# Layer 1's last four output weights: multiplied in the head before the last, and only split in the last one

## The chip, the cores and the metric

The kernel runs on one core of a Trainium2 chip. The metric is the device time of one execution in microseconds (us); less is better. Engines are named as the profile names them: PE (TensorE), DVE (VectorE), ACT (ScalarE), POOL (GpSimd), SP (SyncE, which issues nearly all DMAs here).

## What is computed

Two layers over 1024 latent tokens and 256 context tokens of width 1024. Layer 0 is multi-head latent attention with 16 heads; layer 1, where the change is, is differential attention with 8 heads: each head has two softmaxes over the same values, and the second is subtracted.

```python
def combine(o1, o2, gate):
    o = o1 - lam_full.astype(o1.dtype) * o2
    o = rms_norm(o, g_sub) * (1.0 - lambda_init)
    return gated(o, gate)                    # o * silu(gate)
...
x = layer_norm(DEEPNORM_ALPHA * x + gate[:, None, :] * (o @ out_w[i]), ln_g[i], ln_b[i])
```

In layer 1 only the latent tokens are put out. `gate`, the row behind the attention, is a vector over the 1024 output columns, and g_sub one over the 128 rows of a head's piece of the output weights. So both can be multiplied into the output weights: row k of the weights (128 x 1024, the rows that belong to head k) becomes out_w[k] * gsub * gate1, where gsub is one number per partition and gate1 the gate, repeated on all partitions.

## The kernel before

**Accuracy.** Products are made of split operands: a value is kept as a high part and a low part, and a product is three matmuls (L185 to L187: high by high, low by high, high by low). `split` (L176, L177) casts the high part on ACT and subtracts it on a second engine, DVE or POOL, for the low part; `split16` (L181, L182) does the same in 16 bits with a scale: ACT writes `ph`, `vh`, `kH`, DVE writes `pl`, `vl`, `kL`.

**Layer 1 in heads and tiles.** The loop over the heads h = 0 to 7 runs eight tiles t of 128 queries. A step of a tile computes its scores (`scores1`: matmuls L1338/L1339 into PSUM banks, maxima L1351/L1355 on DVE, six exponentials L1361 on ACT into p0 and p1, then sums and the difference of the softmaxes, L1364 to L1367, on DVE), turns the p of the tile before (`turn1`: transposes L1374, then `split16` into ph and pl) and multiplies the tile before that with the values (`values1`: L1382 to L1384, then o, o2 at L1387/L1388 on ACT, a norm on POOL, and a store of o by SP). Eight PSUM banks "b" are shared by all of it.

**Side work.** Between these pieces a generator G makes the next head's operands: K and Q (`prod_k1`, `prod_q1`, with the buffers rsw, kr, kH, kL, cosB, sinB), V and the head's gate columns (`prod_v1`, with rr, Vf and gg: copies L1316/L1318 from the banks, `split16` of Vf into vh and vl, the silu of gg at L1323, which loads another ACT table, and its store sg_d at L1324), and the next weights. In head 6, the last but one, no weights are left to make; there V of head 7 is woven with rows 0 to 3 of the output weights (`out_w1`): a DMA loads a row into ws (L1421), DVE multiplies it by gsub and gate1 (L1423), and `split` makes the parts oH1k and oL1k.

**The last head.** Before head 7's first tile `out_open` closes the pool a1proj, which holds all the buffers of K, Q, V and the gate, and opens a1out in its place: gb3 (a row of the layer norm), g, res and z (two buffers each), bs and mv. Then it loads gb2 and gb3, takes the space of the layer's input (bigA, bigB) for the parts of rows 4 to 7 ("o1" and "o2" in the trace, `o` where numbers are left out), reads back a tile's o and gate and multiplies them (`out_load`, L1450 to L1452), and for k = 4 to 7 loads a row into z or res (L1421), multiplies it on DVE (L1423) and splits it (ACT L176, POOL L177). In head 7's steps G makes the output of earlier tiles instead: transposes of o (`out_turn`, L1464, split into wx and wy), the product with all eight rows (L185 to L187 with oH, oL), the layer norm and the store. Its first two steps have no such side work.

**What sets the order.** PE executes its instructions in the order of the code. On DVE, ACT, POOL and SP the order is set by the scheduler of the framework, as the rows further down show; every engine, SP's DMA queue too, works through its own order strictly, so that an instruction that waits holds all behind it. A buffer of a closed pool can be written again only when its last readers are done.

Of the kernel before, what the change touches and what calls it, by code (L numbers as in the profile page):

```python
# [17 lines left out]
P = 128  # L18
# [35 lines left out]
def hybrid_kernel(  # L54
# [909 lines left out]
    def bcast_row(dst, src):  # L964
        sp.dma_start(dst, src.to_broadcast([P, D]))
# [9 lines left out]
    def w1(tag):  # L975
        sh, d, b = TAG1[tag]
        return rot(place[tag], sh, d, tag, b)
# [70 lines left out]
    with ow_ctx, spool("o0") as op0:  # L1048
# [96 lines left out]
        for t in range(8):  # L1145
# [53 lines left out]
            "ss": ([P, 2], F32, 2)}  # L1199

    TAGP = {"cosB": ([P, SEQ], F32, 1), "sinB": ([P, SEQ], F32, 1), "rsw": ([P, 512], F32, 1),
            "rr": ([P, 512], F32, 1), "kr": ([P, NTOK], F32, 1),
            "kH": ([P, NTOK], F16, 1), "kL": ([P, NTOK], F16, 1), "gg": ([P, SEQ // P, P], F32, 1),
            "Vf": ([P, NT, P], F32, 1)}

    TAGO = {"gb3": ([P, D], F32, 1), "g": ([P, D], F32, 2), "res": ([P, D], F32, 2), "z": ([P, D], F32, 2),
            "bs": ([P, 2, 6], F32, 2), "mv": ([P, 4], F32, 2)}
    for k_, v_ in TAGL.items():
        rot(wl, v_[0], v_[1], k_, v_[2], first=True)
    prj = ExitStack()  # L1210
    wp = prj.enter_context(spool("a1proj"))
    for k_, v_ in TAGP.items():
        rot(wp, v_[0], v_[1], k_, v_[2], first=True)
# [3 lines left out]
    wo4 = a1.enter_context(spool("a1ow", side="right"))  # L1217
    oHL = [[wo4.tile([P, D], F32R, name=f"oH1{k}"), wo4.tile([P, D], F32R, name=f"oL1{k}")] for k in range(NOW)]
    gate1 = wo4.tile([P, D], F32, name="gate1")
    cosB, sinB = w1("cosB"), w1("sinB")  # L1220

    sp.dma_start(cosB, cs1[0])
# [2 lines left out]
    def weave(main, side, at):  # L1225

        for i, v in enumerate(main):
            if i in at:
                next(side, None)
            yield v  # L1230
        yield from side
# [170 lines left out]
    def gate_row1():  # L1402

        pool.memset(gate1, 0.0)
        sp.dma_start(gate1[0:1, :], ada_b[1:2, 2 * D:3 * D])
        for k in range(KT):
            w = w1("ws")
            sp.dma_start(w, ada_w[1, k * P:(k + 1) * P, 2 * D:3 * D])
            yield 0
            dve.scalar_tensor_tensor(gate1, w, sc[:, 2 * k:2 * k + 1], gate1, op0=ALU.mult, op1=ALU.add)  # L1410
            yield 0
        for c0 in (0, 512):
            bk = bank("b")
            pe.matmul(bk, ones, gate1[:, c0:c0 + 512], start=True, stop=True)
            act.copy(gate1[:, c0:c0 + 512], bk)
            yield 2048

    def out_w1(k, ws_of):

        ws = ws_of()  # L1420
        sp.dma_start(ws, out_w[1, k * P:(k + 1) * P, :])  # L1421
        yield
        dve.scalar_tensor_tensor(ws, ws, gsub, gate1, op0=ALU.mult, op1=ALU.mult)  # L1423
        split(oHL[k][0], oHL[k][1], ws, e_lo=pool)
        yield

    def out_open():

        prj.close()
        wo = a1.enter_context(spool("a1out"))  # L1430
        place.update({k_: wo for k_ in TAGO})
        TAG1.update(TAGO)
        for tag, home, src in (("gb2", "wsq", ln_g), ("gb3", "gb3", ln_b)):
            og[tag] = w1(home)
            bcast_row(og[tag], src[1:2, :])
        rest = [big.tile([P, 5, D], F32R, tag=tg, name=nm("o1")) for tg in ("bigA", "bigB")]
        oHL.extend([r[:, k - NOW, :] for r in rest] for k in range(NOW, KT))
        out_load(0)
        for k in range(NOW, KT):
            z = [w1("z"), w1("res")][k % 2]  # L1440
            for _ in out_w1(k, lambda: z):
                pass
            if k == NOW:
                out_load(1)

    def out_load(t):
# [85 lines left out]
    with tc.manual_schedule(engines={ENG[c] for c in MAN1}):  # L1532
        for _ in prod_q1(0, 0, made.pop("q")):
            pass
        later.pop()()
        for _ in chain(prod_k1(0, made), prod_q1(0, 1),
                       weave(prod_v1(0), prod_w(1, 0), WAT[1])):
            while later:
                later.pop(0)()
        joined, turned = [], []  # L1540

        def step1(cur, side, at):

            with tc.high_priority(HP):
                if cur:
                    S = scores1(*cur)
                    next(S)
            some(side, at[0])
            with tc.high_priority(HP):
                if cur:  # L1550
                    next(S)
                if turned:
                    values1(*turned.pop(0))
            some(side, at[1])
            pc = None
            if joined:
                c_, pc, sm = joined.pop(0)
                ph, pl = w1("ph"), w1("pl")
                turned.append((*c_, ph, pl, sm))
            for (k0, n), v in zip(((0, 4), (4, 4), (8, 2)), at[2:]):  # L1560
                if pc is not None:
                    with tc.high_priority(HP):
                        turn1(pc, ph, pl, k0, n)
                some(side, v)
            if cur:
                with tc.high_priority(HP):
                    joined.append((cur, *next(S)))
            for _ in range(len(later)):
                later.pop(0)()

        g1 = gate_row1()
        part = lambda: (v for _, v in zip(range(4), g1))
        for h in range(H1):
            last = h == H1 - 1
            if not last:
                G = chain(weave(weave(chain(prod_k1(h + 1), prod_q1(h + 1, 0), prod_q1(h + 1, 1)), part(), (1, 9, 17, 25)),
                                prod_w(h + 1, 1), WAT[0]),
                          weave(prod_v1(h + 1), prod_w(h + 2, 0) if h + 2 < H1 else
                                chain(*[out_w1(k, lambda: w1("ws")) for k in range(NOW)]),
                                WAT[1] if h + 2 < H1 else range(1, 40, 4)))  # L1580
            else:
                while later:
                    later.pop(0)()
                out_open()
            for t in range(SEQ // P):
                if last:
                    if t >= 2:
                        out_load(t)
                    G = weave(out_tile1(t - 2), out_turns(t - 1), (9, 12)) if t >= 2 else iter(())
                    if t == 2:  # L1590
                        G = chain(out_turns(0), G)
                    credit[0] = 0
                step1((h, t), G, SLOT1 if not last else SLOTO)
                if last:
                    for _ in G:
                        pass
            for _ in G:
                pass
        for t in range(SEQ // P - 2, SEQ // P):
            G = weave(out_tile1(t), out_turns(t + 1), (9, 12))  # L1600
            credit[0] = 0
            step1(None, G, SLOTO)
            for _ in G:
                pass
# [74 lines left out]
```

## Time and profile before

| | |
|---|---|
| median of 3 runs | 1797.15 us (1794.52 to 1799.22) |
| the profiled execution's own time | 1797.62 us |
| its span in the profile | 1795.8 us (1.8 us lie outside it) |
| mean granted PE clock | 0.988 |
| PE, DVE, ACT, POOL busy | 93%, 69%, 62%, 44% of the span |
| head 6, V of head 7 woven in | about 1586 to 1624 us |
| head 7, the stage of the change | from 1624.6 us |
| first output product of head 7 in full flow | from 1659.5 us |

Rows of the trace give start and duration in us, engine, line, operation, out<-in by the program's names; behind them in brackets stands how long the engine was idle before, and what ended that. Rows of the waits give the waiting engine, tile and line, what it waited for, total, times and longest. Rows of the stretches give, per engine, busy us and instructions, then granted PE clock, DMA share and GB/s.

### The profile page before, as it was taken

The page shows a single profiled execution, that of the slowest core. Times are in us where ns is not written, and L with a number is a line of the kernel's source. Part 1 is how long each engine was busy: PE and PEld are TensorE (multiplying, and loading weights), DVE is VectorE, ACT ScalarE, POOL GpSimd, SP SyncE. Part 2 cuts the span into 40 slices and gives each one's busy share as a digit, 9 for nine tenths or more (in the row PEclk, how much of TensorE's full clock was granted, in tenths as well). Part 3 has the DMA queues.
Part 4 walks back from the last instruction along what each step waited for, and adds up shares of the span by engine and source line. Part 5 has one row for each costly group of instructions (what it writes and reads, how often), then busy time and mean ns, then how long its engine had stood idle before and what let it go on. Part 6 is the DMA issues. An engine that isn't in the chain of part 4 may idle for free. (4 is left out here: it accounts for less than half of the span.)

```text
span 1795.8 us, 36757 instructions
## 1 busy us (share of the span) xinstructions
PE 1668.3 (93%) x14564; PEld 1237.5 (69%) x14564; DVE 1236.9 (69%) x2047; ACT 1117.9 (62%) x2233; POOL 796.3 (44%) x722
## 2 busy tenths in 40 slices
PE   7999989999999998999999999989999999986998
PEld 7999955656666565577866666767676757574876
DVE  7658566566665757557746777787778777979564
ACT  3541167877777787835536676767675766666442
POOL 1422136767776676845541222222314131435454
PEclk9999999999999999999999999999999999998999
DMA  8258520110111112164432213121212122223331
GB/s 304 80 156 256 164 56 23 44 44 21 42 46 34 43 44 81 51 217 161 148 117 74 58 54 79 55 78 54 68 41 64 35 68 58 62 61 124 101 116 70
DMA packets 111225, 154.84 MB, mean 86 GB/s; under 512 B 13415, under 2 KB 84679, under 8 KB 111054
## 3 DMA queue, kind: packets, MB, share of 16 engines
q1 hardware_dynamic: 102654, 144.90, 27.3%
q10 hardware_dynamic: 8400, 7.61, 1.3%
q8 instruction: 114, 1.87, 0.4%
q14 instruction: 57, 0.47, 0.1%
HBM read 98.65 MB, written 27.07 MB: 70 GB/s over the span
## 5 line engine op out<-in xcount | busy, mean ns | idle before, releaser
L779 POOL TENSOR_TENSOR pl<-p,ph 128x1024 f16<-128x1024 f32 (+1 forms) x176 | 364.1, 2074 | 149.3 <-ACT ph L778 122.6
L1361 ACT ACTIVATE p<-ps_b,mx 128x512 f32<-128x512 f32 (+1 forms) x384 | 230.3, 617 | 89.0 <-DVE mx L1357 84.9
L777 ACT ACTIVATE p<-ps_a,esc 128x1024 f32<-128x1024 f32 (+1 forms) x176 | 189.0, 1074 | 93.4 <-PE ps_a L835 87.5
L759 DVE TENSOR_REDUCE mx<-ps_a 128x1 f32<-128x1024 f32 x128 | 155.2, 1222 | 127.7 <-PE ps_a L757 127.7
L778 ACT CAST ph<-p 128x1024 f16<-128x1024 f32 (+1 forms) x176 | 177.1, 1006 | 5.5
L1355 DVE TENSOR_REDUCE mx<-ps_b 128x1 f32<-128x512 f32 x256 | 165.3, 679 | 0.0
L848 PE MATMUL ps_d<-Vh,pl 128*128 128x65 f16 x1344 | 146.0, 194 | 4.5 <-POOL pl L779 4.4
L845 PE MATMUL ps_d<-Vh,ph 128*128 128x65 f16 x1344 | 148.2, 195 | 0.0
L847 PE MATMUL ps_d<-Vl,ph 128*128 128x64 f16 x1344 | 146.9, 193 | 0.0
L1386 POOL TENSOR_TENSOR sm<-sm,us 128x1 f32<-128x1 f32 x64 | 17.9, 280 | 273.6 <-DVE sm L1365 263.5
L1338 PE MATMUL ps_b<-KS,QS 128*128 128x512 f16 (+1 forms) x384 | 125.7, 345 | 12.9 <-DVE pl L182 7.1
L845 PEld LDWEIGHTS <-ph 128*128 128x128 f16 x1344 | 123.3, 97 | 18.0 <-issue 4.6
L847 PEld LDWEIGHTS <-ph 128*128 128x128 f16 x1344 | 123.9, 98 | 12.1
L833 PE MATMUL ps_a<-qH,KH 100*128 100x512 f16 x320 | 121.5, 380 | 8.5 <-ACT p L777 4.2
L1339 PE MATMUL ps_b<-KS,Q 128*128 128x512 f16 (+1 forms) x384 | 129.0, 345 | 0.0
L848 PEld LDWEIGHTS <-pl 128*128 128x128 f16 x1344 | 123.2, 97 | 5.8 <-POOL pl L779 5.8
L181 ACT ACTIVATE ph<-ps_b,lcf 128x512 f16<-128x512 f32 (+1 forms) x192 | 115.1, 647 | 19.3 <-PE ps_b L1374 19.3
L182 DVE SCALAR_TENSOR_TENSOR pl<-ps_b,lcf,ph 128x512 f16<-128x512 f32 (+1 forms) x192 | 117.1, 653 | 13.5 <-ACT ph L181 13.5
L1374 PE MATMUL ps_b<-idr,p 128*128 128x128 f32 x640 | 103.6, 278 | 22.8 <-ACT p L1361 14.7
L834 PE MATMUL ps_a<-qH,KL 96*128 96x512 f16 x320 | 121.3, 379 | 0.0
L835 PE MATMUL ps_a<-qL,KH 96*128 96x512 f16 x320 | 120.7, 377 | 0.0
L1384 PE MATMUL ps_b<-vh,pl 128*128 128x128 f16 x640 | 111.3, 220 | 5.3 <-DVE pl L182 5.3
(427 smaller groups left out, 5261.0 us busy)
## 6 DMA issues: line engine op xcount, KB each, us to landing
ws<-in_dw SPq DMA_DIRECT2D x28, 512.0 KB, 3.9
adw<-in_ada_w SPq DMA_DIRECT2D x24, 512.0 KB, 4.9
adaw<-in_ada_w SPq DMA_DIRECT2D x16, 512.0 KB, 7.4
g<-sg_d SPq DMA_DIRECT2D x16, 512.0 KB, 7.3
sg_d<-gg ACTq DMA_DIRECT2D x40, 128.0 KB, 3.7
o_d<-op SPq DMA_DIRECT2D x7, 640.0 KB, 3.9
xt<-in_xT SPq DMA_DIRECT2D x16, 256.0 KB, 4.4
wgs<-in_w_in SPq DMA_DIRECT2D x32, 128.0 KB, 3.3
```

The lines of the kernel that those rows point to most:

```text
L759: dve.tensor_reduce(mx[:, t, 0:1], ps, axis=AX.X, op=ALU.max)
L777: act.activation(p32[:, :n], st, AF.Exp, scale=esc0)
L778: act.copy(ph[:, :n], p32[:, :n])
L779: pool.tensor_tensor(pl[:, :n], p32[:, :n], ph[:, :n], op=ALU.subtract)
L833: pe.matmul(s_, kh[:nr, ks], QH[:nr, :], start=True, stop=False)
L845: pe.matmul(pv[:, t, :], ph[:, ts], Vh[:, k, h, :], start=(k == kcs[0] and t == 0), stop=False, skip_group_check=True)
L847: pe.matmul(pv[:, t, :V0], ph[:, ts], Vl[:, k, h, :], start=False, stop=False, skip_group_check=True)
L848: pe.matmul(pv[:, t, :], pl[:, ts], Vh[:, k, h, :], start=False, stop=(k == NT - 1), skip_group_check=True)
L1338: pe.matmul(out, qs[m][:, ts], ks[m][:, c0:c0 + n], start=True, stop=False)
L1339: pe.matmul(out, q1[m][:, ts], ks[m][:, c0:c0 + n], start=False, stop=True)
L1355: dve.tensor_reduce(mx[:, 2 + 2 * m + i:3 + 2 * m + i], b, axis=AX.X, op=ALU.max, negate=True)
L1361: act.activation(p[m][:, c0:c0 + n], b, AF.Exp, bias=nb, accum_out=sm[:, 2 + 3 * m + i:3 + 3 * m + i])
```

## The change

The closed pool is split in two. K's and Q's buffers stay in a1proj; rr, gg and Vf go to a new pool a1projv. Both are opened at the start of the layer, but a1proj is closed before V of head 7 (`v_last` in head 6: `out_early`), and z, res, gb3, bs and mv take its place; a1projv is closed where a1proj was (`out_open`), and g takes its place. With z and res there in head 6, `out_pre` loads rows 4 to 7 there and multiplies them: odd rows (res) by gsub on ACT (L1448) and by gate1 on POOL (L1449), even rows (z) by gate1 on POOL only. The loads and multiplications of rows 0 to 3 come twice as densely as before, so that eight rows find room in the weave. In `out_open` only the parts are made: odd rows by `split` (ACT L176, POOL L177), even rows with the scaling in the same step (ACT L1468: high = z * gsub; DVE L1469: low = z * gsub - high). From L1202 on line numbers move; L1361, L1387 and L1423 of before are L1365, L1391 and L1427 of the change.

```diff
--- before.py
+++ after.py
@@ -1199,15 +1199,14 @@
             "ss": ([P, 2], F32, 2)}
 
     TAGP = {"cosB": ([P, SEQ], F32, 1), "sinB": ([P, SEQ], F32, 1), "rsw": ([P, 512], F32, 1),
-            "rr": ([P, 512], F32, 1), "kr": ([P, NTOK], F32, 1),
-            "kH": ([P, NTOK], F16, 1), "kL": ([P, NTOK], F16, 1), "gg": ([P, SEQ // P, P], F32, 1),
-            "Vf": ([P, NT, P], F32, 1)}
-
-    TAGO = {"gb3": ([P, D], F32, 1), "g": ([P, D], F32, 2), "res": ([P, D], F32, 2), "z": ([P, D], F32, 2),
+            "kr": ([P, NTOK], F32, 1), "kH": ([P, NTOK], F16, 1), "kL": ([P, NTOK], F16, 1)}
+    TAGV = {"rr": ([P, 512], F32, 1), "gg": ([P, SEQ // P, P], F32, 1), "Vf": ([P, NT, P], F32, 1)}
+
+    TAGO = {"res": ([P, D], F32, 2), "z": ([P, D], F32, 2), "gb3": ([P, D], F32, 1),
             "bs": ([P, 2, 6], F32, 2), "mv": ([P, 4], F32, 2)}
     for k_, v_ in TAGL.items():
         rot(wl, v_[0], v_[1], k_, v_[2], first=True)
-    prj = ExitStack()
+    prj, prv = ExitStack(), ExitStack()
     wp = prj.enter_context(spool("a1proj"))
     for k_, v_ in TAGP.items():
         rot(wp, v_[0], v_[1], k_, v_[2], first=True)
@@ -1217,6 +1216,11 @@
     wo4 = a1.enter_context(spool("a1ow", side="right"))
     oHL = [[wo4.tile([P, D], F32R, name=f"oH1{k}"), wo4.tile([P, D], F32R, name=f"oL1{k}")] for k in range(NOW)]
     gate1 = wo4.tile([P, D], F32, name="gate1")
+    wv1 = prv.enter_context(spool("a1projv", side="right"))
+    for k_, v_ in TAGV.items():
+        rot(wv1, v_[0], v_[1], k_, v_[2], first=True)
+    place.update({k_: wv1 for k_ in TAGV})
+    TAG1.update(TAGV)
     cosB, sinB = w1("cosB"), w1("sinB")
 
     sp.dma_start(cosB, cs1[0])
@@ -1424,23 +1428,46 @@
         split(oHL[k][0], oHL[k][1], ws, e_lo=pool)
         yield
 
-    def out_open():
+    def out_early():
 
         prj.close()
         wo = a1.enter_context(spool("a1out"))
         place.update({k_: wo for k_ in TAGO})
         TAG1.update(TAGO)
-        for tag, home, src in (("gb2", "wsq", ln_g), ("gb3", "gb3", ln_b)):
-            og[tag] = w1(home)
-            bcast_row(og[tag], src[1:2, :])
+        og["gb3"] = w1("gb3")
+        bcast_row(og["gb3"], ln_b[1:2, :])
+
+    pre = []
+
+    def out_pre(k):
+
+        w = w1(("z", "res")[k % 2])
+        sp.dma_start(w, out_w[1, k * P:(k + 1) * P, :])
+        yield
+        if k % 2:
+            act.activation(w, w, AF.Copy, scale=gsub)
+        pool.tensor_tensor(w, w, gate1, op=ALU.mult)
+        pre.append(w)
+        yield
+
+    def out_open():
+
+        prv.close()
+        wg1 = a1.enter_context(spool("a1outg"))
+        place["g"] = wg1
+        TAG1["g"] = ([P, D], F32, 2)
+        og["gb2"] = w1("wsq")
+        bcast_row(og["gb2"], ln_g[1:2, :])
         rest = [big.tile([P, 5, D], F32R, tag=tg, name=nm("o1")) for tg in ("bigA", "bigB")]
         oHL.extend([r[:, k - NOW, :] for r in rest] for k in range(NOW, KT))
         out_load(0)
-        for k in range(NOW, KT):
-            z = [w1("z"), w1("res")][k % 2]
-            for _ in out_w1(k, lambda: z):
-                pass
-            if k == NOW:
+        for k, w in enumerate(pre):
+            if k % 2:
+                split(*oHL[NOW + k], w, e_lo=pool)
+            else:
+                act.activation(oHL[NOW + k][0], w, AF.Copy, scale=gsub)
+                dve.scalar_tensor_tensor(oHL[NOW + k][1], w, gsub, fv(oHL[NOW + k][0]), op0=ALU.mult, op1=ALU.subtract)
+            if k == 0:
                 out_load(1)
 
     def out_load(t):
@@ -1568,6 +1595,13 @@
             for _ in range(len(later)):
                 later.pop(0)()
 
+        def v_last(h):
+            while later:
+                later.pop(0)()
+            out_early()
+            yield from weave(prod_v1(h), chain(*[out_w1(k, lambda: w1("ws")) for k in range(NOW)],
+                                               *[out_pre(k) for k in range(NOW, KT)]), range(1, 36, 2))
+
         g1 = gate_row1()
         part = lambda: (v for _, v in zip(range(4), g1))
         for h in range(H1):
@@ -1575,9 +1609,7 @@
             if not last:
                 G = chain(weave(weave(chain(prod_k1(h + 1), prod_q1(h + 1, 0), prod_q1(h + 1, 1)), part(), (1, 9, 17, 25)),
                                 prod_w(h + 1, 1), WAT[0]),
-                          weave(prod_v1(h + 1), prod_w(h + 2, 0) if h + 2 < H1 else
-                                chain(*[out_w1(k, lambda: w1("ws")) for k in range(NOW)]),
-                                WAT[1] if h + 2 < H1 else range(1, 40, 4)))
+                          weave(prod_v1(h + 1), prod_w(h + 2, 0), WAT[1]) if h + 2 < H1 else v_last(h + 1))
             else:
                 while later:
                     later.pop(0)()
```

Counted over the layer, DVE loses four multiplications and gains two L1469; ACT gains two scalings, and two of its four casts become scaled copies; POOL gains four multiplications and loses two of four subtractions; no DMA is added, and five (gb3, z, res, z, res) move from the last head to head 6. PE's order is the same.

**ACT, from the end of V to the first exponentials of the last head.** Before: the last copies of V into Vf and gg, the 16-bit high part vh, the silu, o and its square of an earlier tile, the ph of the first turn, and the first exponential.

```order
L1316 COPY Vf_21238<-ps_b_21883 128x128
L1318 COPY gg_21237<-ps_b_21883 128x128
L181 ACTIVATE vh_21239<-Vf_21238,kc_92 128x1280
L1323 ACT_TABLE_LOAD
L1323 ACTIVATE gg_21237<-gg_21237,uw_20924 128x1024
L1387 ACTIVATE o_3348_22039<-ps_b_22008,sm_21606 128x128
L1388 ACTIVATE o_3349_22040,ss_22041<-o_3348_22039 128x128
L181 ACTIVATE ph_22049<-ps_b_22051,lcf 128x512
L181 ACTIVATE ph_22049<-ps_b_22065,lcf 128x256
L181 ACTIVATE ph_22049<-ps_b_22058,lcf 128x512
L1361 ACT_TABLE_LOAD
L1361 ACTIVATE p_3341_21977,sm_21975<-ps_b_21996,mx_21974 128x512
```

Now (o_3352 is the high part of rows 4 to 7):

```order
L1468 ACTIVATE o_3352_21983<-z_21619,gsub 128x1024
L1320 COPY Vf_21283<-ps_b_21930 128x128
L1322 COPY gg_21282<-ps_b_21930 128x128
L181 ACTIVATE vh_21284<-Vf_21283,kc_92 128x1280
L1327 ACT_TABLE_LOAD
L1327 ACTIVATE gg_21282<-gg_21282,uw_20951 128x1024
L176 CAST o_3352_21983<-res_21680 128x1024
L1468 ACTIVATE o_3352_21983<-z_21768,gsub 128x1024
L176 CAST o_3352_21983<-res_21809 128x1024
L181 ACTIVATE ph_22078<-ps_b_22080,lcf 128x512
L181 ACTIVATE ph_22078<-ps_b_22087,lcf 128x512
L1365 ACT_TABLE_LOAD
```

One high part stands ahead of Vf, three stand between the silu and ph, and o with its square has moved behind the exponentials that come next.

**DVE, in the last head.** Before, between the pl of the turn, maxima (mx) and the sums (sm) of a tile, from the first L1367 on:

```order
L1423 SCALAR_TENSOR_TENSOR z_21945<-z_21945,gsub,gate_12517 128x1024
L182 SCALAR_TENSOR_TENSOR pl_22150<-ps_b_22151,lcf,ph_22149 128x512
L182 SCALAR_TENSOR_TENSOR pl_22150<-ps_b_22165,lcf,ph_22149 128x256
L1351 TENSOR_REDUCE mx_22179<-ps_b_22183 128x2
L1355 TENSOR_REDUCE mx_22179<-ps_b_22201 128x1
L1423 SCALAR_TENSOR_TENSOR res_21957<-res_21957,gsub,gate_12517 128x1024
L1423 SCALAR_TENSOR_TENSOR z_21962<-z_21962,gsub,gate_12517 128x1024
L1364 TENSOR_REDUCE sm_22075<-sm_22075 128x2
L182 SCALAR_TENSOR_TENSOR pl_22150<-ps_b_22158,lcf,ph_22149 128x512
L1423 SCALAR_TENSOR_TENSOR res_21969<-res_21969,gsub,gate_12517 128x1024
```

Now the two L1469 stand around the maxima and vl of the first tile (o_3353 is the low part), and the pl of a turn follow one another:

```order
L1355 TENSOR_REDUCE mx_22003<-ps_b_22007 128x2
L1469 SCALAR_TENSOR_TENSOR o_3353_21984<-z_21619,gsub,o_3352_21983 128x1024
L1359 TENSOR_REDUCE mx_22003<-ps_b_22025 128x1
L182 SCALAR_TENSOR_TENSOR vl_21285<-Vf_21283,kc_92,vh_21284 128x1280
L1359 TENSOR_REDUCE mx_22003<-ps_b_22029 128x1
L1359 TENSOR_REDUCE mx_22003<-ps_b_22013 128x1
L1361 TENSOR_SCALAR mx_22003<-mx_22003 128x1
L1359 TENSOR_REDUCE mx_22003<-ps_b_22017 128x1
L1361 TENSOR_SCALAR mx_22003<-mx_22003 128x1
L1469 SCALAR_TENSOR_TENSOR o_3353_21984<-z_21768,gsub,o_3352_21983 128x1024
L182 SCALAR_TENSOR_TENSOR pl_22079<-ps_b_22080,lcf,ph_22078 128x512
L182 SCALAR_TENSOR_TENSOR pl_22079<-ps_b_22087,lcf,ph_22078 128x512
```

The four L1423 are gone from behind the pl, and no multiplication of a weight stands behind the second L1469.

**ACT and SP in head 6.** Before, ACT had o and its square behind the ph of a turn, then a copy of V, then the six exponentials of a tile:

```order
L1387 ACTIVATE o_3247_21350<-ps_b_21319,sm_20941 128x128
L1388 ACTIVATE o_3248_21351,ss_21352<-o_3247_21350 128x128
L1316 COPY Vf_21238<-ps_b_21407 128x128
L1318 COPY gg_21237<-ps_b_21407 128x128
L1361 ACTIVATE p_3260_21439,sm_21438<-ps_b_21447,mx_21437 128x512
L1361 ACTIVATE p_3260_21439,sm_21438<-ps_b_21451,mx_21437 128x512
L1361 ACTIVATE p_3260_21439,sm_21438<-ps_b_21441,mx_21437 128x256
```

Now the same o (o_3272) stands between the exponentials of the tile before, and the scaling of row 5 ahead of those of this tile:

```order
L1320 COPY Vf_21283<-ps_b_21397 128x128
L1322 COPY gg_21282<-ps_b_21397 128x128
L181 ACTIVATE ph_21412<-ps_b_21436,lcf 128x512
L181 ACTIVATE ph_21412<-ps_b_21452,lcf 128x256
L1320 COPY Vf_21283<-ps_b_21445 128x128
L1322 COPY gg_21282<-ps_b_21445 128x128
L1448 ACTIVATE res_21680<-res_21680,gsub 128x1024
L1365 ACTIVATE p_3286_21477,sm_21476<-ps_b_21485,mx_21475 128x512
L1365 ACTIVATE p_3286_21477,sm_21476<-ps_b_21489,mx_21475 128x512
```

On SP the loads follow the store of that o:

```order
L1400 DMA o_d_100<-o_3272_21386 128x128
L965 DMA gb_3254_21280<-in_ln_b 128x1024
L1445 DMA z_21619<-in_out_w 128x1024
L1445 DMA res_21680<-in_out_w 128x1024
L1445 DMA z_21768<-in_out_w 128x1024
L1445 DMA res_21809<-in_out_w 128x1024
L1477 DMA ws_22203<-o_d_100 128x896
L1400 DMA o_d_100<-o_3295_21558 128x128
```

Before, the store stood there followed by the ws<-o_d alone, and the five loads stood behind sg_d of the last head.

## The prediction

> **What bounds the kernel now.** I read the page first, for the busiest engine; then TensorE's waits in the last fifth; then the busy times by stretch around the switch from head 6 to head 7; then single rows there. The page:
>
> ```profile
> span 1795.8 us, 36757 instructions
> PE 1668.3 (93%) x14564; PEld 1237.5 (69%) x14564; DVE 1236.9 (69%) x2047; ACT 1117.9 (62%) x2233; POOL 796.3 (44%) x722
> ```
>
> TensorE is busy 93%, so a change pays only where TensorE stands still, and costs wherever it makes it stand. Its waits from 1480 to 1796 us (total, times, longest), and the stretches (busy time per engine, then granted clock):
>
> ```profile
> PE ps_b L1384 <- DVE pl L182: 5.3, 1, 5.3
> ...
> PE ps_b L187 <- DVE wy L177: 3.8, 1, 3.8
> ```
> ```profile
> 1586.00:1597.00 11.00, 11.00 (x113) 9.40 (x111) 8.60 (x17) 7.01 (x23) 1.64 (x5) 1.00 0.21 49
> ...
> 1629.00:1640.00 11.00, 6.46 (x60) 4.46 (x59) 9.89 (x20) 10.79 (x31) 3.70 (x5) 1.00 0.77 270
> 1640.00:1650.00 10.00, 3.41 (x28) 1.92 (x25) 10.00 (x9) 4.84 (x10) 9.73 (x7) 0.89 0.35 138
> 1650.00:1660.00 10.00, 5.06 (x26) 3.94 (x27) 10.00 (x9) 4.32 (x10) 9.42 (x6) 0.50 0.32 93
> 1660.00:1677.00 17.00, 17.00 (x78) 13.09 (x78) 9.70 (x20) 5.80 (x16) 3.35 (x2) 0.85 0.27 70
> ```
>
> From 1629 to 1660 TensorE idles 4.54 + 6.59 + 4.94 = 16.1 us: the most that this stage can give, the clock aside. Before it TensorE is full, and after 1660 it is full again, so the end of the wait at L187 sets the end of the span. What holds it there (first the chain of waits, then VectorE):
>
> ```profile
> 1628.97 3.19 DMA sg_d<-gg
> ...
> 1632.67 6.34 DMA z<-in_out_w
> ```
> ```profile
> 1637.17 1.55 DVE L1367 SCALAR_TENSOR_TENSOR p<-p,sm,p 128x1280 f32<-128x1280 f32 x1
> 1639.03 2.72 DVE L1423 SCALAR_TENSOR_TENSOR z<-z,gsub,gate 128x1024 f32<-128x1024 f32 x1 [0.31 <-DMA z<-in_out_w]
> ...
> 1643.92 2.37 DVE L1423 SCALAR_TENSOR_TENSOR res<-res,gsub,gate 128x1024 f32<-128x1024 f32 x1
> 1646.21 3.37 DVE L1423 SCALAR_TENSOR_TENSOR z<-z,gsub,gate 128x1024 f32<-128x1024 f32 x1
> ...
> 1650.23 2.64 DVE L1423 SCALAR_TENSOR_TENSOR res<-res,gsub,gate 128x1024 f32<-128x1024 f32 x1
> ...
> 1653.46 1.64 DVE L1366 SCALAR_TENSOR_TENSOR sm<-sm,nlam 128x1 f32<-128x1 f32 x1
> ...
> 1655.21 3.67 DVE L1367 SCALAR_TENSOR_TENSOR p<-p,sm,p 128x1280 f32<-128x1280 f32 x1
> 1658.81 0.68 DVE L177 TENSOR_TENSOR wy<-ps_b,wx 128x512 fp32r<-128x512 f32 x1
> ```
>
> Row 4 of the output weights (z) is only issued behind the stored gate, and lands at 1639.03. Four multiplications stand on VectorE between the pieces of attention: 2.72 + 2.37 + 3.37 + 2.64 = 11.1 us. The pl behind them holds TensorE for 5.3 us; L1367, 3.67 us beside POOL's split where it is 1.55 at 1637.17, delays wy, and that the output product.
>
> **The change, part by part: the gain.** Out of the last head go the four L1423, 11.1 us on VectorE. In come two L1469 (bounded by the 1.55 of L1367 and the 3.37 of the slowest L1423) early in it. POOL's splits fall from four to two. The four hi parts of ScalarE remain, but as the order shows one stands ahead of the last Vf, and three between the gate's silu and the first exponentials, where two o and a third ph stood. ScalarE there before, and TensorE:
>
> ```profile
> 1624.79 0.27 ACT L1316 COPY Vf<-ps_b 128x128 f32<-128x128 f32 x1 [0.18 <-PE ps_b L187]
> ...
> 1627.79 1.15 ACT L1323 ACTIVATE gg<-gg,uw 128x1024 f32<-128x1024 f32 x1
> 1628.85 0.35 ACT L1387 ACTIVATE o<-ps_b,sm 128x128 f32<-128x128 f32 x1
> ...
> 1629.60 1.61 ACT L181 ACTIVATE ph<-ps_b,lcf 128x512 f16<-128x512 f32 x3
> 1631.23 1.28 ACT L1361 ACT_TABLE_LOAD   x1
> 1632.52 0.69 ACT L1361 ACTIVATE p<-ps_b,mx 128x512 f32<-128x512 f32 x1
> ...
> 1641.78 1.04 ACT L176 CAST o<-z 128x1024 fp32r<-128x1024 f32 x1 [1.12 <-DVE z L1423]
> ...
> 1643.98 0.47 ACT L1361 ACTIVATE p<-ps_b,mx 128x256 f32<-128x256 f32 x1
> ```
> ```profile
> 1631.47 0.27 PE L1338 MATMUL ps_b<-KS,QS 128*128 128x256 f16 x1 [1.78 <-DVE pl L182]
> 1638.87 1.28 PE L1374 MATMUL ps_b<-idr,p 128*128 128x128 f32 x10 [2.34 <-ACT o L1388]
> 1650.37 0.29 PE L1384 MATMUL ps_b<-vh,pl 128*128 128x128 f16 x1 [5.29 <-DVE pl L182]
> 1652.05 1.70 PE L1464 MATMUL ps_b<-idr,ws 128*128 128x128 f32 x7
> 1654.49 0.79 PE L185 MATMUL ps_b<-oH,wx 128*128 128x512 f32 x1 [0.74 <-ACT wx L176]
> 1659.54 0.80 PE L187 MATMUL ps_b<-oH,wy 128*128 128x512 f32 x1 [3.84 <-DVE wy L177]
> ```
>
> With the cast's 1.04 for a hi part, walk down the new order. The first hi part pushes Vf and all behind it by 1.0, so silu ends near 1629.8. Three hi parts end at 1632.8, two ph (two thirds of 1.61) at 1633.9, the table load at 1635.2: the exponentials start 2.7 us later than at 1632.52. The pl at the head of the stage needs that ph, and VectorE is then in the second L1469 until about 1634.3, so L1338 starts at some 1635.0, not at 1631.47: this wait grows from 1.8 to 5.3 us. The transposes of p (1638.87) start near 1642.0, 3.1 late.
>
> From here the loss turns: no L1423 stands between the pl, so the values, which waited to 1650.37 and ended at 1652.05, end at about 1647.0, 5 us early. The transposes of o (1.70) and the casts of wx (0.74) give the first L185 at 1649.4; L185 and its twin L186 take some 1.2 (0.79 busy each, overlapping). The other input is wy: the last exponentials of tile 1 ended 5.6 us behind the transposes of p (1638.87 to 1644.45), so now at 1647.6; then the sums and L1367 (2.4 from the end of the exponentials to 1638.72 before) and wy's 0.6, at 1650.6. Both meet there, and L187 runs at about 1650.6 instead of 1659.54: 8.9 us. Two terms stand against each other. The stretch from 1660 had 0.85 of the clock, 0.15 x 17 = 2.5 us lost, which a TensorE that no longer stands in front of it gets back. Half clock behind the new 5.3 us wait (the 5.29 before is followed by a stretch at 0.50) costs between nothing, if the tile waits there anyway, and the same 2.5; I take 0.9, since waits remain around it. And POOL's ws*g (L1452, quoted with the POOL rows below) now falls beside L1367 and may stretch it by 0 to 2.6; I take the middle, 1.3. Gain: 8.9 + 2.5 - 0.9 - 1.3 = 9.2 us, with bounds at 8.9 - 0.9 - 2.6 = 5.4 (no clock back, full stretch) and 8.9 + 2.5 = 11.4.
>
> [...]
>
> **The change, part by part: the cost in head 6.** Five DMAs (gb3 and rows 4 to 7) move ahead of the attention's last tiles, on SP behind a store of o; ScalarE gets two scalings, POOL four multiplications, in a stretch where TensorE is full (11.00 of 11.00). What they touch:
>
> ```profile
> 1598.68 0.69 ACT L1361 ACTIVATE p<-ps_b,mx 128x512 f32<-128x512 f32 x1 [2.90 <-DVE mx L1357]
> ...
> 1602.15 0.23 ACT L1361 ACTIVATION_READ_ACCUMULATOR p<-ps_b,mx 128x1 f32 x1
> ```
> ```profile
> 1596.35 0.33 SPq L1396 DMA_DIRECT2D o_d<-o  x1
> ```
> ```profile
> 1637.86 2.81 POOL L1452 TENSOR_TENSOR ws<-ws,g 128x896 f32<-128x896 f32 x1 [0.64 <-DMA g<-sg_d]
> ...
> 1648.45 3.34 POOL L177 TENSOR_TENSOR o<-res,o 128x1024 fp32r<-128x1024 f32 x1
> ...
> 1655.20 2.34 POOL L177 TENSOR_TENSOR o<-res,o 128x1024 fp32r<-128x1024 f32 x1
> ```
>
> ScalarE works in order, and the scaling of row 5 (res) stands right ahead of the exponentials that began at 1598.68. Those are six in a row, to 1602.15, with TensorE full on both sides, so a delay of theirs beyond a few tenths of a microsecond is a delay of TensorE. The store of o ahead of the loads (1596.35 before) comes earlier too, its two o now standing between the exponentials of the two halves; I put the loads at 1593, row 5 third among them at 1594. Its landing time is the unknown: z before took 6.34 with more loads beside it (270 GB/s over that stretch), so row 5 lands between 1598.3 (two thirds of that) and 1600.3. Plus 1.04 the exponentials start at 1599.4 to 1601.4, 0.7 to 2.7 late. The second scaling, behind the next exponentials, falls into idle time like the 2.90 above, if row 7 has landed. POOL's multiplications (2.34 each, as the split of the same shape) have 9 us of idle POOL in 11, but two would lie beside the next L1366 and L1367, for 0 to 1.3 more. I take 2.2 us (the upper part of the first, a third of the second), with bounds at 0 (the loads land early) and 5 (the large toll, below).
>
> [...]
>
> Sum against the profiled execution (1797.62, of which the span is 1795.8): 1797.62 - 9.2 + 2.2 = 1790.6. The median is 0.47 below it, within the runs' own scatter, so I leave it: 1790.6 us.
>
> **The rivals.** *A large toll in head 6.* For it: SP's store waits for POOL's chain; if it stays at 1596.35, row 5 is issued near 1597.7 and lands at 1604, and the exponentials start at 1605.1, 6.4 late; halfway between that and my 2.2, with part of POOL's stretch, is a toll of 5. Against: the order has the o earlier. 1797.62 - 9.2 + 5 = 1793.4. *A new wait in place of the old.* The hi parts ahead of the exponentials, the half clock that stays to the output product, and a full stretch of L1367: the gain's lower bound, 1797.62 - 5.4 + 2.2 = 1794.4. For it: ScalarE is busy 10.79 of 11.00 there already. Against: VectorE loses 11.1 us right behind. *Slower: ScalarE held by a load.* Every microsecond that row 5 lands later than about 1597.6 is one on TensorE; from a landing at about 1607 on (1597.6 + 9.2), 13 us behind its issue, the change loses. With the store at 1596.35 and a landing 12.5 us later the toll is 12.6: 1797.62 - 9.2 + 12.6 = 1801.0. Against: the 6.34 of z in the busiest stretch for loads. *It doesn't do what it says.* If the closed buffers come free only with the last head's, the loads wait and all stays as it was: 1797.6. Against: rr, gg and Vf, which live to the end of V, are out of that pool.
>
> **How the numbers follow.** The forecast has 0.53, the large toll 0.22, the new wait 0.11, slower 0.09, no effect 0.05. The range is 1785.5 (the whole 11.4 and no toll give 1786.2, less half a microsecond of the runs' scatter) to 1799.0, which leaves out most of the slower case. Below 0.3% (5.4 us, about what a measurement of this kernel can tell from no change), so under 1791.8: most of the forecast and the small ends of two rivals, 0.53; within it: the rest of these, 0.38; slower by more: 0.09.
>
> **What would show it.** Right: TensorE's 5.3 and 3.8 us waits at L1384 and L187 gone; one wait of about 5 at L1338 near the head of the last head; L1384 no longer behind L1423; a PEclk near 1.00 in the output product; and one wait of 1 to 3 us on ScalarE's p in head 6, behind a scaling of res. Wrong: TensorE waits in several tiles of head 6, row 5 landing over 8 us behind its issue, L1367 of 3 us or more there, or the L1338 wait over 8 us.

## The result, and the profile after

| | runs | median, us (range) | against before, fast runs |
|---|---|---|---|
| before | 15 | 1798.07 (1794.52 to 1802.19) | |
| the change | 15 | 1791.24 (1786.93 to 1795.16) | 0.9958 [0.9950, 0.9967] |
| the change, a second series (change_again) | 5 | 1790.89 (1788.17 to 1792.94) | 0.9956 [0.9943, 0.9968] |

The change makes the kernel 0.42% faster: 7.6 us, with an interval of 5.9 to 9.0. The forecast was 1790.6, a gain of 7.0. The page of the profiled execution (1792.78 us):

```profile
span 1790.9 us, 36759 instructions
PE 1664.6 (93%) x14564; PEld 1232.2 (69%) x14564; DVE 1228.9 (69%) x2045; ACT 1119.1 (62%) x2235; POOL 797.3 (45%) x724
```

TensorE has 3.7 us less of busy time for the same 14564 matmuls: they ran at a higher mean clock (0.991 against 0.988). That sum alone shows little, since two executions of one program further down, load_order and load_order_again, differ by 6.3 us in it (1663.6 and 1669.9). To find what the change did, the two executions are cut at instructions that both have. The whole span can't be compared directly: the first wait of head 6, ahead of anything that the change touches, ends at 1576.37 before and at 1578.24 here. The cuts are the first transposes of the tile before which row 5's scaling stands, the last matmul of V, and the first L187 of the output product that runs on. Before, and then with the change:

```profile
1576.37 0.90 PE L1374 MATMUL ps_b<-idr,p 128*128 128x128 f32 x3 [4.72 <-DVE p L1367]
...
1599.66 0.60 PE L1374 MATMUL ps_b<-idr,p 128*128 128x128 f32 x4
...
1624.48 0.27 PE L187 MATMUL ps_b<-wy,h1L 128*128 128x256 f16 x1
```
```profile
1578.24 1.11 PE L1378 MATMUL ps_b<-idr,p 128*128 128x128 f32 x4 [4.71 <-DVE p L1371]
...
1601.36 0.60 PE L1378 MATMUL ps_b<-idr,p 128*128 128x128 f32 x4
...
1628.03 0.27 PE L187 MATMUL ps_b<-wy,h1L 128*128 128x256 f16 x1
...
1638.85 0.69 PE L1378 MATMUL ps_b<-idr,p 128*128 128x128 f32 x2 [5.83 <-DVE pl L182]
...
1648.02 1.29 PE L1378 MATMUL ps_b<-idr,p 128*128 128x128 f32 x10 [3.07 <-DVE p L1371]
...
1656.24 0.50 PE L185 MATMUL ps_b<-oH,wx 128*128 128x512 f32 x1 [0.64 <-ACT wx L176]
...
1657.09 0.50 PE L187 MATMUL ps_b<-oH,wy 128*128 128x512 f32 x1
```

| us, one profiled execution each | end of head 6 (transposes to last V) | stage (last V to L187) | tail (L187 to the span's end) | sum |
|---|---|---|---|---|
| before | 24.82 | 35.06 | 136.26 | 196.14 |
| the change | 26.67 | 29.06 | 133.81 | 189.54 |
| change_again | 26.49 | 28.42 | 133.72 | 188.63 |
| load_order | 24.82 | 27.63 | 133.75 | 186.20 |
| load_order_again | 24.81 | 29.67 | 133.73 | 188.21 |
| pool_scales | 24.81 | 27.94 | 133.75 | 186.50 |
| dve_multiplies | 26.01 | 28.93 | 133.77 | 188.71 |
| late_splits | 26.35 | 33.68 | 136.98 | 197.01 |
| late_splits_dve | 26.28 | 28.81 | 136.08 | 191.17 |
| early_loads_only | 24.82 | 32.69 | 135.74 | 193.25 |
| two_and_two | 24.81 | 26.15 | 134.44 | 185.40 |

So the change pays 1.85 us in head 6, gains 6.00 in the stage and 2.45 behind it, 6.6 in sum. (The expectations below measure the first part from the wait near 1577 us, 48.11 before and 49.79 with the change; that piece holds a stretch of half clock whose length varies between executions, a mean granted clock of 0.84 from 1575 to 1586 us in the two and of 0.69 in change_again, and the 24.82 does not.) The stretches of the change, to be held against those of before:

```profile
1597.00:1608.00 11.00, 9.75 (x97) 8.04 (x95) 6.02 (x13) 7.24 (x21) 7.88 (x5) 1.00 0.62 240
...
1629.00:1640.00 11.00, 5.17 (x50) 3.85 (x49) 10.42 (x14) 10.94 (x15) 5.92 (x4) 0.80 0.37 104
1640.00:1650.00 10.00, 6.93 (x56) 4.64 (x55) 7.84 (x13) 8.05 (x26) 7.09 (x7) 0.84 0.41 161
1650.00:1660.00 10.00, 9.24 (x63) 6.11 (x61) 7.70 (x17) 5.87 (x19) 2.80 (x6) 0.86 0.03 10
1660.00:1677.00 17.00, 17.00 (x108) 13.51 (x108) 11.33 (x22) 7.33 (x20) 5.10 (x6) 1.00 0.30 90
```

The stretch from 1597 before is this:

```profile
1597.00:1608.00 11.00, 11.00 (x112) 9.40 (x109) 8.00 (x16) 6.58 (x23) 1.56 (x4) 1.00 0.20 55
```

There are 1.25 us of idle TensorE in head 6 that were not there, and 9.7 us instead of 16.1 from 1629 to 1660. In the stretch from 1660 the clock is 1.00 instead of 0.85, and TensorE does 108 matmuls in 17 us instead of 78.

The toll in head 6 (the 1.85 us) comes from one place. ScalarE, with the change:

```profile
1601.19 1.15 ACT L1448 ACTIVATE res<-res,gsub 128x1024 f32<-128x1024 f32 x1 [3.70 <-DMA res<-in_out_w]
1602.25 0.67 ACT L1365 ACTIVATE p<-ps_b,mx 128x512 f32<-128x512 f32 x1
...
1639.08 0.69 ACT L1365 ACTIVATE p<-ps_b,mx 128x512 f32<-128x512 f32 x1
```

The scaling of row 5 waits 3.70 us for its load (issued by SP at 1594.84, so 6.35 us on the way), and the exponentials behind it start at 1602.25. Before, they started at 1598.68. The transposes just ahead were 1.70 us late already (1601.36 against 1599.66), so the exponentials start 1.87 us later than that accounts for. TensorE then waits for their p in two places:

```profile
1603.06 0.66 PE L1378 MATMUL ps_b<-idr,p 128*128 128x128 f32 x4 [0.45 <-ACT p L1365]
...
1604.85 0.27 PE L185 MATMUL ps_b<-wx,h1H 128*128 128x256 f16 x1 [0.79 <-ACT p L1365]
```

The L185 at 1604.85 stood at 1601.30 before: 3.55 us later, of which 1.70 were there already, so 1.85 is the toll. (The last row of ScalarE above, the first exponential of the last head, is for further down.)

### The profile page after: what moved, and what is told of

Its sections match the earlier page's. It is cut to its first block, busy times and chain, and to the rows that moved or that the text cites. A ratio compares the mean times of both kernels' runs of the same rounds, so it can differ in the third digit from the quotient of the medians.

```text
span 1790.9 us, 36759 instructions
## 1 busy us (share of the span) xinstructions
PE 1664.6 (93%) x14564; PEld 1232.2 (69%) x14564; DVE 1228.9 (69%) x2045; ACT 1119.1 (62%) x2235; POOL 797.3 (45%) x724
## 3 DMA queue, kind: packets, MB, share of 16 engines
q8 instruction: 114, 1.87, 0.5%
## 5 line engine op out<-in xcount | busy, mean ns | idle before, releaser
L1365 ACT ACTIVATE p<-ps_b,mx 128x512 f32<-128x512 f32 (+1 forms) x384 | 230.4, 617 | 85.0 <-DVE mx L1361 83.4
L1342 PE MATMUL ps_b<-KS,QS 128*128 128x512 f16 (+1 forms) x384 | 127.9, 350 | 10.7 <-DVE pl L182 5.0
L1378 PE MATMUL ps_b<-idr,p 128*128 128x128 f32 x640 | 103.4, 277 | 30.3 <-ACT p L1365 15.4
L1378 PEld LDWEIGHTS ps_b<-idr,p 128*128 128x128 f32 x640 | 77.5, 142 | 56.5 <-ACT p L1365 23.7
```

What stands on the lines that cost most here:

```text
L1342: pe.matmul(out, qs[m][:, ts], ks[m][:, c0:c0 + n], start=True, stop=False)
L1365: act.activation(p[m][:, c0:c0 + n], b, AF.Exp, bias=nb, accum_out=sm[:, 2 + 3 * m + i:3 + 3 * m + i])
L1378: pe.transpose(st[:, j * P:(j + 1) * P], pc[:, (k0 + j) * P:(k0 + j + 1) * P], idn)
```

## Experiments

**load_order.** What makes the toll?

```diff
-  *[out_pre(k) for k in range(NOW, KT)]), range(1, 36, 2))
+  *[out_pre(k) for k in (4, 6, 5, 7)]), range(1, 36, 2))
```

(`pre` is kept by k, so that `out_open` finds its rows in the old order.)

> Rows 4 to 7 are loaded and multiplied in the order 4, 6, 5, 7 instead of 4, 5, 6, 7; nothing else. In the order of ScalarE both scalings of odd rows then stand behind the six exponentials of the tile, not ahead of them; loads, multiplications and engines are the same. Measured from the 4.7 us wait for p near 1577 us to the last V matmul: 48.11 us in the kernel before, 49.79 with the change, a toll of 1.68. Theory (the toll is the exponentials standing in ScalarE's queue behind a scaling that waits for its load): toll 0 to 0.3, time about 1.6 us under the change's. Rival (the toll is POOL's four multiplications beside VectorE, or the five loads): toll stays 1.4 to 2.

ScalarE at the same place:

```profile
1599.73 0.69 ACT L1365 ACTIVATE p<-ps_b,mx 128x512 f32<-128x512 f32 x1 [2.20 <-DVE mx L1361]
...
1603.54 1.18 ACT L1448 ACTIVATE res<-res,gsub 128x1024 f32<-128x1024 f32 x1
```
```profile
1597.00:1608.00 11.00, 11.00 (x110) 9.38 (x108) 7.95 (x15) 8.70 (x26) 8.04 (x4) 1.00 0.62 243
```

The exponentials again wait only for their maxima, the scaling follows them, and TensorE is full, while POOL's work (8.04 us) and the loads (243 GB/s) are much the same as in the changed kernel (7.88 and 240). The longer segment is 48.07, the shorter 24.82: the toll is gone entirely. The rival falls. 1788.99 us in 4 runs, ratio 0.9955 [0.9940, 0.9970].

**pool_scales.** Is it ScalarE's queue, or POOL's work beside VectorE?

```diff
-  act.activation(w, w, AF.Copy, scale=gsub)
+  pool.tensor_scalar(w, w, gsub, None, op0=ALU.mult)
```

> The scaling of rows 5 and 7 by gsub moves from ScalarE to POOL (two more POOL instructions of 128x1024 in head 6), nothing else. Theory of the ScalarE queue: toll in head 6 down from 1.68 to 0 to 0.4, the rest as with the change, time about 1.5 us under the change's. [...]

Longer segment 48.06, shorter 24.81, although POOL was busy 10.56 of the 11 us from 1597 to 1608:

```profile
1597.00:1608.00 11.00, 11.00 (x112) 9.40 (x110) 8.53 (x17) 7.21 (x24) 10.56 (x4) 1.00 0.40 161
```

So POOL's work in head 6 costs TensorE nothing here, and the queue on ScalarE is the whole toll. 1788.18 us in 10 runs, ratio 0.9949 [0.9934, 0.9964].

**dve_multiplies.** Does it matter which engine multiplies? (The code is shortened.)

```diff
 def out_pre(k): ...
-  if k % 2:
-      act.activation(w, w, AF.Copy, scale=gsub)
-  pool.tensor_tensor(w, w, gate1, op=ALU.mult)
 def out_open(): ...
-  if k % 2: ...                               # both branches, the parts as the change makes them
+  dve.scalar_tensor_tensor(w, w, gsub, gate1, op0=ALU.mult, op1=ALU.mult)
+  split(*oHL[NOW + k], w, e_lo=pool)          # all four rows
```

The multiplication is written in `out_open`, but stands in VectorE's order in head 6, where its row has landed.

> The four multiplications of rows 4 to 7 stay on VectorE in one instruction each (gsub and gate1), but run in head 6 on the early loads; in the last head all four rows are split by ScalarE's cast and POOL's subtraction, as before. VectorE has the first one ahead of the tile's negated maximum, so the exponentials hang on two loads through VectorE. If the gain of the last head comes from taking the multiplications out of it, whichever engine does them, the stretch from the last V matmul to the first output product that runs on (35.06 us before, 29.06 with the change) is 28 to 31 here, with POOL's four splits against two. If it comes from spreading them over ScalarE and POOL, it is over 32. The toll in head 6: 1 to 4 us, as the loads now hold VectorE. Time: 1 to 3 us over the change's.

Stage 28.93, tail 133.77, toll 1.19 by the shorter segment. By this one execution the gain doesn't depend on which engine multiplies, as long as it is not done in the last head. The time was not 1 to 3 us over the change's; the sum of the three parts, 188.71, lies between the two executions of the change. 1789.22 us in 10 runs, ratio 0.9962 [0.9949, 0.9975].

**early_loads_only.** As dve_multiplies, with `gsub` replaced by `gl`; the multiplications and splits now stand behind the first tile's step of the last head, and the second tile's `out_load` ahead of them (shortened):

```diff
+  gl = wo4.tile([P, 2], F32, name="gl")
+  dve.scalar_tensor_tensor(gl[:, 0:1], sm[:, 4:5], 0.0, gsub, op0=ALU.mult, op1=ALU.add)
+  dve.scalar_tensor_tensor(w, w, gl[:, 0:1], gate1, op0=ALU.mult, op1=ALU.mult)
```

> Rows 4 to 7 and gb3 are loaded in head 6 as with the change, but multiplied on VectorE in the last head (one instruction of gsub and gate1 per row, as before; gsub is passed through a tiny value of the first tile's sums, so that they can't run earlier), then cast on ScalarE and subtracted on POOL as before. Separates the early load from the early multiplication. Theory (the VectorE work in the last head is what holds TensorE; the load hides): toll 0 to 0.3, the stretch from the last V matmul to the first output product that runs on stays at 32 to 36 us (before 35.06), and the tail behind it at about 136 with half clock. Rival (the load of row 4 behind the gate's store held it all): 31 or less, tail 134.

VectorE in the stage:

```profile
1641.94 3.12 DVE L1468 SCALAR_TENSOR_TENSOR z<-z,gl,gate 128x1024 f32<-128x1024 f32 x1
1644.98 1.27 DVE L1468 SCALAR_TENSOR_TENSOR res<-res,gl,gate 128x1024 f32<-128x1024 f32 x1
1646.17 3.09 DVE L1468 SCALAR_TENSOR_TENSOR z<-z,gl,gate 128x1024 f32<-128x1024 f32 x1
1649.19 1.27 DVE L1468 SCALAR_TENSOR_TENSOR res<-res,gl,gate 128x1024 f32<-128x1024 f32 x1
```
```profile
1650.91 0.59 PE L1342 MATMUL ps_b<-KS,QS 128*128 128x512 f16 x1 [6.16 <-DVE pl L182]
...
1660.56 0.50 PE L187 MATMUL ps_b<-oH,wy 128*128 128x512 f32 x1 [3.10 <-DVE wy L177]
```

Stage 32.69, toll 0, tail 135.74. As the theory had it, both old waits are back, 6.16 us behind the multiplications and 3.10 at L187. So of the change's gain behind V (8.45 us) 2.9 come with the early load and 5.6 with the early multiplication, by one execution each, which is loose by up to 2 us (see change_again). One time only: 1798.04, beside a run range of 1794.59 to 1803.60 of the kernel before.

**late_splits.** Is the new wait of 5.8 us made by the high parts on ScalarE? Four rows as here, emitted behind the second tile's step, and the second tile's `out_load` ahead of them (shortened):

```diff
+  dve.scalar_tensor_tensor(gl[:, 0:1], pl[:, 9, 0:1], 0.0, gsub, op0=ALU.mult, op1=ALU.add)
+  dve.tensor_scalar(gl[:, 1:2], pl[:, 9, 0:1], 0.0, 1.0, op0=ALU.mult, op1=ALU.add)
-  act.activation(hi, w, AF.Copy, scale=gsub)          # even rows; odd rows: cast
+  act.activation(hi, w, AF.Copy, scale=gl[:, 0:1])    # even rows; odd rows: gl[:, 1:2], which is 1
```

> The four high parts of the last head are made to wait for the low part of the first tile's turned p (their scale is a tiny value worked out from it), so they stand in ScalarE's queue behind the exponentials of the last head's second tile instead of ahead of those of its first; o and its square and the third ph return to their old place. The same work otherwise, two tiny VectorE instructions more. Theory (ScalarE's queue of high parts makes the new wait of 5.8 us at L1378): that wait falls to about 2, the exponentials start 8 us behind the last V matmul as before the change, not 11, and the stretch from the last V matmul to the first output product is 25 to 27.5 instead of 29.06, limited by the high parts that now stand ahead of the casts of wx. Rival (the wait is VectorE's L1469 and POOL's splits, not the high parts): the wait stays over 4. Time 2 to 4 us under the change's, with the clock at most at half for less time.

TensorE's waits in the last head:

```profile
PE ps_b L1378 <- DVE p L1371: 5.8, 1, 5.8
PE ps_b L187 <- DVE wy L177: 5.0, 1, 5.0
PE ps_b L1342 <- DVE pl L182: 2.2, 1, 2.2
PE ps_b L185 <- ACT o L1391: 1.7, 1, 1.7
```

The wait for pl is down from 5.8 to 2.2, at L1342 as before the change, and the exponentials start 8.24 us behind the last V matmul: that half of the theory holds. But the stage is 33.68, not 25 to 27.5, the tail starts at half clock again (0.50 from 1658 to 1668 us), and the ratio 1.0003 [0.9993, 1.0013]: the whole gain is lost. VectorE and POOL show where:

```profile
1642.57 3.48 DVE L1371 SCALAR_TENSOR_TENSOR p<-p,sm,p 128x1280 f32<-128x1280 f32 x1
...
1654.83 3.05 DVE L1371 SCALAR_TENSOR_TENSOR p<-p,sm,p 128x1280 f32<-128x1280 f32 x1
1657.81 3.35 DVE L1478 SCALAR_TENSOR_TENSOR o<-z,gsub,o 128x1024 fp32r<-128x1024 f32 x1
```
```profile
1642.63 2.07 POOL L1486 TENSOR_TENSOR ws<-ws,g 128x896 f32<-128x896 f32 x1
...
1654.19 5.89 POOL L1475 TENSOR_TENSOR o<-res,o 128x1024 fp32r<-128x1024 f32 x2
```

These VectorE instructions on two operands in SBUF take 1.27 to 1.55 us by themselves and 3.05 to 3.48 here, beside a POOL instruction. With the change, POOL's subtractions (1634.71 to 1640.34) run while VectorE mostly reads PSUM (mx 0.68 us, two pl 1.40); only one L1469 falls beside them, 2.05 us long. Late, they run beside p and the low parts.

**late_splits_dve.** The same, with the odd rows' low parts on `dve.tensor_tensor` in place of `pool.tensor_tensor`.

> As late_splits, but the low parts of the odd rows are made on VectorE instead of POOL, so that POOL's two subtractions do not run beside VectorE's p and low parts. In late_splits L1371 took 3.05 us beside them (1.55 alone), the second L1478 3.35 (1.27 alone). Theory (POOL's instruction beside a VectorE instruction with two operands in SBUF makes VectorE wait): both back to 1.3 to 1.6, two more VectorE instructions of about 1.3 ahead of wy, so the stretch from the last V matmul to the first output product 33.68 - 1.5 - 2.1 + 2.5 = 32.6 (32 to 33.5). Rival (those were slow for another reason): L1371 stays at 3, stretch 35 to 36.5.

```profile
1641.97 1.55 DVE L1371 SCALAR_TENSOR_TENSOR p<-p,sm,p 128x1280 f32<-128x1280 f32 x1
...
1651.98 1.55 DVE L1371 SCALAR_TENSOR_TENSOR p<-p,sm,p 128x1280 f32<-128x1280 f32 x1
1653.44 1.28 DVE L1478 SCALAR_TENSOR_TENSOR o<-z,gsub,o 128x1024 fp32r<-128x1024 f32 x1
```
```profile
1642.03 3.44 POOL L1486 TENSOR_TENSOR ws<-ws,g 128x896 f32<-128x896 f32 x1
```

The second L1371 and the second L1478 are back to their price alone, so their stretch came from POOL's subtractions. The stage is 28.81, under the expected 32 to 33.5: the first L1371 lost its stretch as well (3.48 to 1.55), which I had not counted. POOL's multiplication of o runs beside it in both kernels, but in late_splits POOL's L1486 took 2.07 beside the 3.48, and here 3.44 beside the 1.55. The edit touches neither instruction, so 1.9 us of the 4.9 that the stage fell look like luck; no run separates this. The three parts sum to 191.17, still 1.6 over the change's. One time: 1794.54.

**two_and_two.** Rows 4 and 5 as in the change with load_order; rows 6 and 7 gated in the same way, by a value of wy's first half, with both low parts on VectorE.

> Load order as in load_order (toll gone); rows 4 and 5 are split where the change splits them, rows 6 and 7 only behind the first low part of wy (their scale is a tiny value worked out from it), with both low parts on VectorE, so two high parts fewer stand ahead of the last head's first exponentials, and one POOL subtraction fewer stands beside VectorE. Theory (each high part ahead of the exponentials is about 1.05 us on the path): the exponentials 2.1 us earlier behind the last V matmul than with the change, the stretch to the first output product 25 to 26.5 (load_order 27.63), toll 0; the tail 133.8 if rows 6 and 7 come in time for the product, up to 135 if TensorE waits for their parts. Time 1.5 to 2.5 us under load_order's. Rival (late rows are missed by the product): the tail grows by what the stretch gains, no gain.

The wait for pl fell to 3.54 us (5.83 with the change), the exponentials start 9.07 us behind the last V matmul (11.05), and the stage fell to 26.15, inside the 25 to 26.5 and below every other, by one execution; the tail is 134.44, 0.7 more than load_order's 133.75. 1787.98 us in 6 runs, ratio 0.9940 [0.9920, 0.9960].

**change_again and load_order_again**, side by side:

> The changed kernel as it is, on the same chip as load_order_again, for a direct comparison. Segments as in its first profile: toll 1.68, stretch 29.06, tail 133.8; ratio to before 0.996.

> load_order as it is. From the segments (48.07 + 27.63 + 133.75 against 49.79 + 29.06 + 133.81) it is 3.2 us faster than the change: ratio to before 0.9945 against 0.996 for change_again beside it. If the gain of its segments is given back outside them, the two ratios agree.

Head 6 repeats (26.49 against 24.81). The stage does not: 28.42 against 29.67, where it was 29.06 against 27.63. The same program thus moves by 0.6 to 2.0 us in the stage from one execution to the next, up to as much as the toll; where that comes from stands in the last section. Ratios 0.9956 [0.9943, 0.9968] and 0.9953 [0.9938, 0.9968]: that load_order, pool_scales and two_and_two beat the change is not shown by these times, only that their head 6 has no toll. That both beat the kernel before is shown.

## Why the prediction was right

**The gain, 9.2 forecast, 8.45 measured (6.00 + 2.45).** The clock's 2.5 us came out at 2.45: in all kernels whose L187 isn't waited for by more than 0.3 us the tail is 133.7 to 133.8 (134.4 with the late rows), and in the four with a wait of 1.7 to 5.0 there it is 135.7 to 137.0. The half clock in the product goes with the wait ahead of it in all eleven executions: in the first piece of the product behind it, most matmuls of L185 to L187 take 0.63 us each in the four and 0.39 or 0.40 in the other seven. The exponentials were to start 2.7 us later behind the last V matmul and start 3.0 later (1639.08 - 1628.03 = 11.05 against 8.04). The wait of 5.3 at L1338 came as 5.83 at L1378, the two last transposes, one bank earlier in TensorE's order than I had put it. The waits of 5.29 us (L1384) and 3.84 us (L187) are gone.

**The step that was too small**: the transposes of the first tile's p were to be 3.1 late and are 5.6 late (19.99 us behind the last V matmul against 14.39). The sums stood behind four maxima, whose scores TensorE had made mostly at half clock (0.50 from 1640 to 1642, 0.76 in the microsecond behind), and POOL's multiplication of o did not stretch L1367 (L1371 now) but the tiny L1366 (L1370):

```profile
1641.56 2.61 DVE L1359 TENSOR_REDUCE mx<-ps_b 128x1 f32<-128x512 f32 x4
...
1644.09 0.15 DVE L1368 TENSOR_REDUCE sm<-sm 128x2 f32<-128x6 f32 x1
...
1644.58 1.70 DVE L1370 SCALAR_TENSOR_TENSOR sm<-sm,nlam 128x1 f32<-128x1 f32 x1
1646.32 1.56 DVE L1371 SCALAR_TENSOR_TENSOR p<-p,sm,p 128x1280 f32<-128x1280 f32 x1
```

1.70 where it is 0.22 alone: 1.5 us, which the 1.3 of the forecast covered by size, not by place. Together the stage came to 29.06 where the terms gave 28.4 (35.06 - 8.9 + 0.9 + 1.3).

That the last leg fits is partly luck. From the transposes to L187 the forecast had 8.6 us: 5.6 to the end of tile 1's exponentials, then 3.0 for the sums, the difference p and wy. It came to 9.07, but as 3.4 and 5.6:

```profile
1650.95 0.48 ACT L1365 ACTIVATE p<-ps_b,mx 128x256 f32<-128x256 f32 x1
```
```profile
1652.65 0.69 DVE L1359 TENSOR_REDUCE mx<-ps_b 128x1 f32<-128x512 f32 x1 [1.44 <-PE ps_b L1343]
...
1656.35 0.69 DVE L177 TENSOR_TENSOR wy<-ps_b,wx 128x512 fp32r<-128x512 f32 x1
```

The sums stood behind a maximum that waited for scores, which the forecast did not have. And the 0.9 for half clock was put behind the wait for pl; a second drop, to 0.50 behind the wait for p at 1648.02, cost about 1.5 us by itself (9.07 us from there to L187 against 7.54 in change_again, last section).

What the sum held as one term, the early load and the early multiplication, is about a third load and two thirds multiplication by early_loads_only, within its looseness of 2 us.

**The toll, 2.2 forecast, 1.85 measured.** Its mechanism was right in each step: third load, 6.35 us on the way, scaling, exponentials 1.87 late (0.7 to 2.7 forecast). No run shows the part of it that I gave to POOL beside VectorE in head 6, 0 to 1.3: pool_scales has six POOL instructions there and no toll. Without its third of that, 0.43, the 2.2 is 1.77, which is about the middle of 0.7 to 2.7 and not its upper part. TensorE's one wait of 1 to 3 us on ScalarE's p came as two, 0.45 and 0.79.

**The rivals.** The large toll and the slower case needed row 5 to land at 1604 or later; it landed at 1601.2 (1599.5 on the clock of the execution before, 1.70 earlier), and the store of o went out at 1593.00, as the order had it. The new wait in place of the old did appear, 5.83 us long and with half clock behind it, but the old ones behind it were worth more, and the clock was back for the product. Which of the two happens is decided by little: late_splits cuts this new wait to 2.2 us, and loses all.

## What to carry to other kernels

Where TensorE is full, look at what stands in an in-order queue between the work that it waits for: one scaling that waits for a load, placed ahead of six exponentials, cost 1.85 us, and exchanging two loads took it away. Work that is taken off the critical engine can be paid for where it goes; here the early high parts look like the next thing to move, but moving all four put POOL's subtractions beside VectorE's own two-operand work, 3.05 and 3.35 us where it takes 1.55 and 1.27 alone, and gave everything back. For effects of a few microseconds in 1800, cut the span at instructions that both kernels have: the executions were up to 6.7 us apart (1576.0 to 1582.8) ahead of the places that the edits touch.

## What the hardware showed that I had not expected

The clock fell behind a shorter wait than I had reckoned with. I had put half clock behind the new wait alone, 5.83 us long as it came. With the change the granted clock dropped at 1635.64, inside that wait, and again at 1649.30, behind the wait of 3.07 us for p; it was back at 1642.48 and 1652.72 (all four worked out from its mean in one-microsecond stretches). At the second drop TensorE, idle from 1644.95 to 1648.02, had been at work again for 1.28 us:

```profile
1647.00:1648.00 1.00, 0.00 (x0) 0.01 (x1) 0.87 (x1) 0.09 (x1) 1.00 (x1) 1.00 0.00 0
1648.00:1649.00 1.00, 0.98 (x9) 1.00 (x10) 0.00 (x0) 1.00 (x3) 0.90 (x3) 1.00 0.00 0
1649.00:1650.00 1.00, 1.00 (x8) 0.79 (x7) 0.59 (x1) 1.00 (x3) 0.17 (x2) 0.65 0.11 33
1650.00:1651.00 1.00, 1.00 (x4) 0.30 (x2) 1.00 (x3) 1.00 (x4) 0.00 (x0) 0.50 0.12 33
```

So the length of a wait alone does not tell whether it costs clock, and the same program comes out either way. The change's wait of 3.07 us at the transposes of p was followed by half clock, change_again's of 3.00 was not; load_order_again's of 2.54 was, load_order's of 2.20 and two_and_two's of 2.89 were not. What decides it was not shown. From these transposes to L187 it takes 7.53 to 7.54 us in change_again, load_order, pool_scales and two_and_two, where the ten transposes take 1.28 to 1.29 us and each score matmul of 512 columns behind them 0.38. It takes 9.00 to 9.16 in the change, load_order_again and dve_multiplies, where half clock fell on them: 0.63 for most of these score matmuls in the change, and 2.37 and 1.90 for the transposes in the other two. That is 1.5 us, most of the 2.0 by which load_order's stage varied. The change's own stage varied by 0.64 only, since in change_again the transposes came 0.89 later behind the last V matmul.
